# Three dense PSUM banks in a hybrid encoder kernel, with the retention's scores and outputs in one bank

## The chip, the cores and the metric

The kernel runs on one core of a Trainium2 chip. A core has five engines with a queue of instructions each: TensorE (PE in the profile; its weight loads are shown apart, as PEld), VectorE (DVE), ScalarE (ACT), GpSimd (POOL) and SyncE (SP), which issues the DMAs here. Each engine takes its instructions in the order of its queue. An instruction can wait for semaphores that other engines or DMAs raise. TensorE writes its products into PSUM, a memory of eight banks; a bank holds 512 columns of 32-bit floats on each of 128 partitions. VectorE and ScalarE read the products there.

The metric is the device time of one execution in microseconds (us): the median over the runs.

## The reference, cut to what matters

Two layers are computed over 2048 tokens of width 1024. Each normalizes its input, projects it to eight parts of 512 columns, runs two kinds of heads, and adds the projected result to the input.

```python
def hybrid_layer(x, norm_gain, w_in, w_out, rel_bias, cos, sin):
    hn = rms_norm(x, norm_gain)
    proj = hn @ w_in
    aq, ak, av, ag, rq, rk, rv, rg = jnp.split(proj, cuts, axis=-1)
    ya = chunked_rel_attention(aq, ak, av, rel_bias)      # 8 heads x 64, softmax over 9 chunks of 64
    yr = chunkwise_retention(rq, rk, rv, cos, sin)        # 4 heads x 128
    y = concatenate([ya * silu(ag), yr * silu(rg)])
    return x + y @ w_out

def chunkwise_retention(q, k, v, cos, sin):               # q, k turned by rotary phases
    att = einsum("bnihd,bnjhd->bnhij", qc, kc) * intra_decay     # scores, masked with decays
    o_intra = einsum("bnhij,bnjhe->bnihe", att, vc)
    kv = einsum("bnjhd,hj,bnjhe->bnhde", kc, k_decay, vc)
    state = state * chunk_decay + kv                             # carried from chunk to chunk
    o_inter = einsum("bnihd,hi,bnhde->bnihe", qc, q_decay, states)
    return rms_norm(o_intra + o_inter)
```

## The kernel before, in words

**Precision.** Every large operand is held as two 16-bit floats, an upper part and a remainder (`h` and `l`). A product of two such operands takes three TensorE instructions: upper by upper, upper by remainder, remainder by upper.

**Tiles and stages.** A layer is worked through in four groups `s` (one retention head and two attention heads each), and a group in four stages `n` of 512 tokens. A stage has two dense parts. `dense_T` makes four sections `j` of 128 transposed columns (attention's q and k, retention's q and k): 24 products of 128x512 each, into one PSUM tile per section. `dense_V` makes the untransposed columns (v, gates, retention's v) for four blocks `a` of 128 tokens: 24 products of 128x512 each. After the four groups `wout` does the output projection with the same shape of product (line 1105) into the same pool of banks.

**Steps.** All these are Python generators that yield after eight wide products. `run` goes around them. At each step it lets the dense generator issue its products, then calls `tick`, which issues what an earlier step had put off with `later(k, ...)` until k steps on, then lets `attention` issue its part, then pulls work from a list of background generators (the preparation of the next group's weights, the first layer's norms). The order on the four compute engines' queues is the order in which the Python code issues. Attention of stage n runs beside the dense parts of stage n+1, in eight units (four blocks `a`, two heads `hx`) of three steps.

**The retention in these steps.** Unit (a, 1) issues the attention scores S (lines 800, 801) at its first step. At its second step `decayed` issues three products of 128x128 (line 860): the retention's scores of block a+1, or of the next stage's block 0. At its third step `retention` issues the outputs of block a: six products into columns 0 to 127 and three, the addition to the state, into columns 128 to 255. With `tick`, VectorE multiplies the scores by the decay mask one step after they were issued (line 880), ScalarE makes the upper half of the masked scores two steps after (line 864), VectorE the remainder three steps after (line 868). After the outputs, VectorE adds to the state one step on (line 908), ScalarE squares the outputs for the norm two steps on (line 929, into columns 256 to 383 of the same tile), VectorE and GpSimd make the root three steps on, and VectorE the normalized, gated result four steps on (line 925).

**PSUM.** Eight banks: pool `psD` has two for the dense sections, `psS` one tile of two banks for attention's scores, `psR` four for everything small: attention's outputs `o` (line 817), the retention's scores `r1` (line 873), its outputs `r2` (line 891), the sums over columns that the weight preparation takes (`allsum`, line 322) and the start's transposes. A pool hands out its banks in turn; the first write to a tile waits until the last reader of the tile that had the bank before is done. So a section of `dense_T` or `dense_V` waits for the reading of the section two before it; the last reader of a `dense_V` section is VectorE's gate (line 770).

**The first group's tokens.** In the first layer's first group the transposed tokens of stage n+1 are made while stage n runs: for each of four blocks of 128 tokens a norm, a split into upper half and remainder, and two transposing DMAs (lines 236 and 237), by the generator `norms_from_input` and, for the second stage, a list written out by hand. A wide product of `dense_T` reads all four blocks. Stage (0, 0, 0) alone has its first two sections in column parts (line 712): products of 128 columns, one block of tokens at a time.

Of the kernel before, what the change touches and what calls it, by code (L numbers as in the profile page):

```python
# [10 lines left out]
F32 = mybir.dt.float32  # L11
I32 = mybir.dt.int32
AF = mybir.ActivationFunctionType
ALU = mybir.AluOpType
AX = mybir.AxisListType
PSUM = bass.MemoryType.PSUM
DRAM = bass.MemoryType.DRAM

P = 128
# [8 lines left out]
def hybrid_trunk(ctx: ExitStack, tc: tile.TileContext, x, pos, gain, gcol, w_in, w_out, rel, fgain,  # L28
# [4 lines left out]
    KT = D // P  # L33
# [3 lines left out]
    act, dve, pool, pe, sp = nc.scalar, nc.vector, nc.gpsimd, nc.tensor, nc.sync  # L37
# [8 lines left out]
    w4 = ctx.enter_context(tc.tile_pool(name="w4", bufs=3))  # L46
    gp = ctx.enter_context(tc.tile_pool(name="gp", bufs=5))
    dp = ctx.enter_context(tc.tile_pool(name="dp", bufs=1, space=DRAM))
    psD = ctx.enter_context(tc.tile_pool(name="psD", bufs=2, space=PSUM))
    psS = ctx.enter_context(tc.tile_pool(name="psS", bufs=1, space=PSUM))  # L50
    psR = ctx.enter_context(tc.tile_pool(name="psR", bufs=4, space=PSUM))


    warm = cp.tile([P, 1], F32, tag="warm", name="warm")
# [146 lines left out]
    ring = {}  # L201
# [393 lines left out]
    def later(k, fn):  # L595
        deferred.append([k, fn])
# [11 lines left out]
    def dense_T(l, s, n, g, st):  # L608
        hh, hl = hT[l, n]
        nm = f"{l}_{s}_{n}"  # L610
        st.tabc = b1.tile([P, 512], F32, tag="tabc", name=f"tabc{nm}")
        st.tabs = b1.tile([P, 512], F32, tag="tabs", name=f"tabs{nm}")
        def tab_load():
            while n not in tab_done:
                pull(1)
            sp.dma_start(st.tabc, tab_d[n][0])
            sp.dma_start(st.tabs, tab_d[n][1])

        first = (l, s, n) == (0, 0, 0)
# [85 lines left out]
        if first:  # L705
            ps = [psD.tile([P, 512], F32, tag="dense", name=f"dT{nm}_{j}") for j in range(2)]
            for (j, a) in ((0, 0), (0, 1), (0, 2), (1, 0), (1, 1), (1, 2), (0, 3), (1, 3)):
                cs = slice(a * P, (a + 1) * P)
                m = 0
# [5 lines left out]
            for j in range(2):  # L715
                evacuate(j, ps[j])
                yield
        for j in range(2 if first else 0, 4):
            if j == 2 and not first:
                tab_load()  # L720
            if first:
                ps = psR.tile([P, 512], F32, tag="small", name=f"dT{nm}_{j}")
            else:
                ps = psD.tile([P, 512], F32, tag="dense", name=f"dT{nm}_{j}")
            while g.tdone <= j:
                pull(1)
            m = 0
            terms = ((g.h, hh), (g.l, hh), (g.h, hl))
            order = [(kt, w) for w in terms for kt in range(KT)] if j == 0 else [(kt, w) for kt in range(KT) for w in terms]
            for kt, (w_, h_) in order:  # L730
                pe.matmul(ps, w_[:, j, kt, :], h_[:, kt, :], start=(m == 0), stop=(m == 23))  # L731
                m += 1
                if m in (8, 16) or (m == 24 and first):
                    yield
            evacuate(j, ps)
            yield
# [41 lines left out]
    def attention(l, s, n, g, st, prev, nxt):  # L778
# [61 lines left out]
        for i, (a, hx) in enumerate(units):  # L840
            flow(1)
            u = qk(a, hx)
            yield
            if hx == 1:
                if a < 3:
                    decayed(l, s, n, g, st, a + 1)
                elif nxt is not None:
                    decayed(*nxt, 0)
            yield
            if hx == 1:  # L850
                next(ret, None)
            elif a == 0 and (l, s, n) == (0, 0, 0):
                decayed(l, s, n, g, st, 0)
            pipe.append(lambda u=u: pv(u))
            yield


    def products(out_, pairs):
        for i, (w_, m_) in enumerate(pairs):
            pe.matmul(out_, w_, m_, start=(i == 0), stop=(i + 1 == len(pairs)))  # L860

    def upper_of(dst, src):

        act.activation(dst[:, 0], src, AF.Copy, scale=2.0 ** -11)

    def rest_of(dst, src):

        dve.scalar_tensor_tensor(out=dst[:, 1], in0=dst[:, 0], scalar=-2.0 ** 11, in1=src, op0=ALU.mult, op1=ALU.add)

    def decayed(l, s, n, g, st, a):  # L870
        nm = f"{l}_{s}_{4 * n + a}"
        cs = slice(a * P, (a + 1) * P)
        r1 = psR.tile([P, 512], F32, tag="small", name=f"r1{nm}")
        products(r1[:, 0:P], [(st.rk[:, i, cs], st.rq[:, j, cs]) for i, j in ((0, 0), (0, 1), (1, 0))])

        def upper():
            st.dT = b1.tile([P, 2, P], F16, tag="dT", name=f"dT{nm}")
            upper_of(st.dT, r1[:, P:2 * P])

        later(1, lambda: dve.tensor_tensor(r1[:, P:2 * P], r1[:, 0:P], g.msk, op=ALU.mult))  # L880
        later(2, upper)
        later(3, lambda: rest_of(st.dT, r1[:, P:2 * P]))

    def retention(l, s, n, g, st):
        for a in range(4):
            t = 4 * n + a
            nm = f"{l}_{s}_{t}"
            cs = slice(a * P, (a + 1) * P)
            last = t == NT - 1
            dT = st.dT  # L890
            r2 = psR.tile([P, 512], F32, tag="small", name=f"r2{nm}")
            rv = st.rv[a]
            terms = [(dT[:, 0], rv[:, 0]), (dT[:, 0], rv[:, 1])]
            if t > 0:
                sh = ring["halves"]
                terms += [(st.rq[:, 0, cs], sh[:, 0]), (st.rq[:, 1, cs], sh[:, 0]), (st.rq[:, 2, cs], sh[:, 1])]
            products(r2[:, 0:P], terms + [(dT[:, 1], rv[:, 2])])
            if not last:
                kh, kl = st.kt[:, a, :], st.kt[:, 4 + a, :]
                products(r2[:, P:2 * P], [(kh, rv[:, 0]), (kh, rv[:, 1]), (kl, rv[:, 0])])  # L900
                if t == 0:
                    ring["state"] = b1.tile([P, P], F32, tag="state", name=f"state{nm}")
                ns = ring["state"]
                sh = ring["halves"] = b1.tile([P, 2, P], F16, tag="sh", name=f"sh{nm}")

                def add(r2=r2, ns=ns, t=t):
                    if t > 0:
                        dve.scalar_tensor_tensor(out=ns, in0=r2[:, P:2 * P], scalar=2.0 ** (-7 - s), in1=ns,
                                                 op0=ALU.mult, op1=ALU.add)
                    else:  # L910
                        dve.tensor_scalar(ns, r2[:, P:2 * P], 2.0 ** (-7 - s), None, op0=ALU.mult)

                later(1, add)
                later(2, lambda sh=sh, ns=ns: upper_of(sh, ns))
                later(3, lambda sh=sh, ns=ns: rest_of(sh, ns))
                later(5, lambda ns=ns: act.activation(ns, ns, AF.Copy, scale=(1.0 - 2.0 ** (-5 - s)) ** P))
            ss = b2.tile([P, 1], F32, tag="rss", name=f"rss{nm}")

            def root(ss=ss):
                dve.tensor_scalar(ss, ss, g.ra[:, 0:1], g.re[:, 0:1], op0=ALU.mult, op1=ALU.add)  # L920
                pool.tensor_tensor(ss, ss, mhalf, op=ALU.pow)

            def fin(t=t, a=a, r2=r2, ss=ss, nm=nm):
                y = b1.tile([P, P], F32, tag="yr", name=f"yr{nm}")
                dve.scalar_tensor_tensor(out=y, in0=r2[:, 0:P], scalar=ss[:, 0:1], in1=st.g[a][:, P:256],
                                         op0=ALU.mult, op1=ALU.mult)
                sp.dma_start(y_d[t][:, 512 + s * P:512 + (s + 1) * P], y)

            later(2, lambda r2=r2, ss=ss: act.activation(r2[:, 2 * P:3 * P], r2[:, 0:P], AF.Square,
                                                         accum_out=ss))  # L930
            later(3, root)
            later(4, fin)
            yield
# [197 lines left out]
    def pull(k):  # L1131
        for _ in range(k):
            while bg:
                try:
                    next(bg[0][0])
                    bg[0][1] -= 1
                    break
                except StopIteration:
                    bg.pop(0)
# [7 lines left out]
    def grp(l, s):  # L1147
        if (l, s) not in groups:
            groups[l, s] = Grp()
        return groups[l, s]  # L1150
# [146 lines left out]
    spare = [h_.rearrange("p k c -> p (k c)")[:, i * 2 * D:(i + 1) * 2 * D] for h_ in far[1] for i in range(2)]  # L1297
    xk = [Tok(t, xs0[t], None) if t < 4 else Tok(t, late[t - 4], spare[t - 4]) for t in range(8)]
    d0 = dense_T(0, 0, 0, g00, st0)
    g00.vh = b3.tile([P, KT, 512], F16, tag="wh", name="whV0_0")  # L1300
    g00.vl = b3.tile([P, KT, 512], F16, tag="wl", name="wlV0_0")
# [69 lines left out]
    for l in range(DEPTH):  # L1371
        gO = [Grp(), Grp()]
        go = Grp()
        for s in range(NSW):
            g = grp(l, s)
            for n in range(NS):
                first = (l, s, n) == (0, 0, 0)
                if not first:
                    st = states.setdefault((l, s, n), St())
                    dT = dense_T(l, s, n, g, st)  # L1380
                else:
                    st = st0
# [42 lines left out]
                m = n + 1 if n + 1 < NS else 0  # L1425
# [90 lines left out]
```

## Time and profile before

| | us |
|---|---|
| median of 3 runs (lowest, highest) | 2094.98 (2092.48, 2095.95) |
| the profiled execution | 2094.75 |
| its span, from the first to the last instruction | 2092.8 |
| TensorE busy | 2004.4 (96%) |
| VectorE busy | 1343.8 (64%) |
| ScalarE busy | 1141.3 (55%) |
| GpSimd busy | 432.9 (21%) |
| DMA queue q1, share of 16 engines | 66.4% |
| mean granted TensorE clock | 0.991 |

The profile names a group of instructions by line, engine, operation and tiles written and read (out<-in). The name `r` stands for both tiles of the retention, `r1` and `r2`, since numbers are left out; products that read `rot` only are scores, those that begin with `rv,dT` are outputs. In a group's row stand the count, the busy time in us, the mean duration of one in ns, and the idle time of the engine just before these instructions with what ended most of it. In the order of time a row begins with the start and the duration in us; in square brackets stands the idle time before it and what released it.

### The profile page before, as it was taken

The numbers are of one execution on the slowest core, as the hardware profiler recorded it, in microseconds if no ns is written. First come the engines' busy times: TensorE is split into PE (matmuls) and PEld (weight loads), VectorE is DVE, ScalarE is ACT, GpSimd is POOL, SyncE is SP. The second block draws the span as 40 slices with busy tenths as digits, with TensorE's granted clock in tenths as the row PEclk, the third lists the DMA queues.
The fourth block names the chain that finished last, engine by engine and source line by source line (L and its number), as shares of the span: only waits on it lengthen the run. The fifth ranks groups of instructions, "written<-read, shape, count | busy, mean of one in ns | idle before, by whom it ended". The sixth has DMA issues, their size and how long they took to land.

```text
span 2092.8 us, 39599 instructions
## 1 busy us (share of the span) xinstructions
PE 2004.4 (96%) x14014; PEld 1049.4 (50%) x14014; DVE 1343.8 (64%) x4031; ACT 1141.3 (55%) x2522; POOL 432.9 (21%) x509
## 2 busy tenths in 40 slices
PE   6888999999999999998999999999999999998998
PEld 4344455555555555444444555555555555554443
DVE  7676666666656666576654666666666667656643
ACT  7455665556565654455444546554655565455432
POOL 1022222222122212121000222222222222222100
PEclk9999999999999999999999999999999999999999
DMA  8767674557476764599965556655655776558874
GB/s 247 171 127 162 136 166 114 115 112 159 110 169 133 161 166 99 113 211 260 219 185 113 120 102 142 130 121 106 155 123 118 178 156 162 117 100 183 212 199 123
DMA packets 645702, 313.65 MB, mean 150 GB/s; under 512 B 459232, under 2 KB 602080, under 8 KB 645504
## 3 DMA queue, kind: packets, MB, share of 16 engines
q1 hardware_dynamic: 645504, 311.12, 66.4%
q8 instruction: 110, 1.80, 0.4%
q14 instruction: 88, 0.72, 0.1%
HBM read 123.26 MB, written 41.98 MB: 79 GB/s over the span
## 4 chain that ended last, share of the span: by engine, by line
PE 55%; DMA 7%; DVE 5%; ACT 3%; issue 1%; SPq 1%; POOL 0%; POOLq 0%; DVEq 0%; ACTq 0%
PE dT L731 18%; PE dV L752 15%; PE dO L1105 12%; DMA pT<-pq 2%; PE r L860 2%; PE S L801 2%; PE S L800 2%; PE o L820 1%; PE o L821 1%; PE o L822 1%; DVE sc L804 1%; DMA swp<-rot 1%; DMA yhy<-rhy 1%; ACT sc L807 1%; ACT pq L809 1%
## 5 line engine op out<-in xcount | busy, mean ns | idle before, releaser
L810 POOL TENSOR_TENSOR pq<-sc,pq 128x640 f16<-128x640 f32 (+4 forms) x256 | 323.8, 1265 | 1175.9 <-issue 590.7
L807 ACT ACTIVATE sc<-sc,mq,cT 128x640 f32<-128x640 f32 (+4 forms) x256 | 218.5, 853 | 558.1 <-DVE mq L806 413.7
L752 PE MATMUL dV<-whV,hTh 128*128 128x512 f16 x1024 | 354.5, 382 | 13.0 <-DVE gt L770 12.8
L731 PE MATMUL dT<-hTh,whT 128*128 128x512 f16 x1008 | 349.4, 382 | 14.7 <-DMA hTh<-hTl 9.6
L752 PE MATMUL dV<-wlV,hTh 128*128 128x512 f16 x1024 | 354.1, 381 | 0.0
L752 PE MATMUL dV<-whV,hTl 128*128 128x512 f16 x1024 | 354.0, 381 | 0.0
L731 PE MATMUL dT<-hTl,whT 128*128 128x512 f16 x1008 | 346.6, 379 | 0.0
L731 PE MATMUL dT<-hTh,wlT 128*128 128x512 f16 x1008 | 346.6, 379 | 0.0
L752 PEld LDWEIGHTS <-hTh 128*128 128x128 f16 x2048 | 197.3, 98 | 227.7 <-DVE gt L770 16.4
L731 PEld LDWEIGHTS <-whT 128*128 128x128 f16 x2016 | 192.9, 98 | 221.6 <-issue 24.1
L804 DVE CUSTOM_DVE_ANT_0 sc<-S,bias 128x640 f32<-128x640 f32 (+4 forms) x256 | 188.4, 736 | 78.8 <-PE S L801 61.1
L1105 PE MATMUL dO<-whO,yly 128*128 128x512 f16 x512 | 194.1, 379 | 2.4 <-DMA yly<-rly 2.4
L1105 PE MATMUL dO<-whO,yhy 128*128 128x512 f16 x512 | 194.0, 379 | 1.2 <-DVE gt L770 0.6
L1105 PE MATMUL dO<-wlO,yhy 128*128 128x512 f16 x512 | 194.0, 379 | 0.0
L809 ACT ACTIVATE pq<-sc 128x640 f16<-128x640 f32 (+4 forms) x256 | 171.5, 670 | 10.9 <-DMA pT<-pq 3.0
L1105 PEld LDWEIGHTS <-yhy 128*128 128x128 f16 x1024 | 99.6, 98 | 115.1 <-issue 0.8
L752 PEld LDWEIGHTS <-hTl 128*128 128x128 f16 x1024 | 99.7, 98 | 105.0 <-issue 2.8
L800 PE MATMUL S<-k,q 128*128 128x128 f16 (+3 forms) x592 | 143.1, 268 | 7.9 <-DVE mq L804 7.9
L731 PEld LDWEIGHTS <-wlT 128*128 128x128 f16 x1008 | 97.2, 98 | 101.8 <-issue 1.1
L820 PE MATMUL o<-v,pT 128*128 128x65 f16 x1120 | 129.6, 193 | 10.2 <-DMA pT<-pq 9.7
L801 PE MATMUL S<-k,q 128*128 128x128 f16 (+3 forms) x592 | 130.5, 268 | 0.0
L820 PEld LDWEIGHTS <-pT 128*128 128x128 f16 x1120 | 105.3, 97 | 49.2 <-DMA pT<-pq 21.3
(350 smaller groups left out, 3352.7 us busy)
## 6 DMA issues: line engine op xcount, KB each, us to landing
q<-qq SPq DMA_DIRECT2D x128, 128.0 KB, 2.7
yyy<-y_d SPq DMA_DIRECT2D x32, 512.0 KB, 4.6
stT<-in_w_in_dram SPq DMA_DIRECT2D x27, 512.0 KB, 4.8
stV<-in_w_in_dram SPq DMA_DIRECT2D x26, 512.0 KB, 4.5
k<-kk SPq DMA_DIRECT2D x128, 64.0 KB, 2.0
swp<-rot SPq DMA_DIRECT2D x64, 128.0 KB, 2.5
tabc<-tab SPq DMA_DIRECT2D x32, 256.0 KB, 2.7
tabs<-tab SPq DMA_DIRECT2D x32, 256.0 KB, 2.9
```

Of the source, the lines that this page charges most:

```text
L731: pe.matmul(ps, w_[:, j, kt, :], h_[:, kt, :], start=(m == 0), stop=(m == 23))
L752: pe.matmul(ps, h_[:, kt, a * P:(a + 1) * P], w_[:, kt, :], start=(m == 0), stop=(m == 23))
L800: pe.matmul(o, st.q[:, hx, 0, cs], k_, start=True, stop=False)
L801: pe.matmul(o, st.q[:, hx, 1, cs], k_, start=False, stop=True)
L804: dve.tensor_tensor_reduce(out=v, in0=S[:, 0:w], in1=g.bias[hx][:, 640 - w:640], scale=1.0, scalar=-3.0e38, op0=ALU.add, op1=ALU.max, accu ...
L807: act.activation(v, v, AF.Exp, bias=m[:, 0:1], scale=g.c[:, 0:1])
L809: act.activation(pq[:, 0:w], v, AF.Copy)
L810: pool.tensor_tensor(pq[:, w:2 * w], v, pq[:, 0:w], op=ALU.subtract)
L820: pe.matmul(o[:, 0:65], u.p[:, b, :], v_[:, 0:65], start=(b == 0), stop=False)
L821: pe.matmul(o[:, 0:64], u.p[:, b, :], v_[:, 65:129], start=False, stop=False)
L860: pe.matmul(out_, w_, m_, start=(i == 0), stop=(i + 1 == len(pairs)))
L1105: pe.matmul(ps, h_[:, kt, :], w_[:, kt, :], start=(m == 0), stop=(m == 23))
```

## The change

The pool `psD` gets a third bank and `psR` loses its fourth. The retention's outputs of block a no longer take a bank of their own: they go into the bank that the scores of block a+1 were given one step before, kept in `ring["rr"]`. The scores move to its last 128 columns and are masked in place; the outputs keep columns 0 to 383. Only the very last block's outputs take a new bank.

In the first group of the first layer, the stages n = 1, 2 and 3 compute the first two sections of `dense_T` in column parts: for each of the four token blocks, 24 products of 128x128 for section 0 and then 24 for section 1, into two dense banks that are held side by side. They yield every 32 products, so that the count of steps stays at twelve a stage. Both sections are evacuated after the last block.

```diff
-    psD = ctx.enter_context(tc.tile_pool(name="psD", bufs=2, space=PSUM))
+    psD = ctx.enter_context(tc.tile_pool(name="psD", bufs=3, space=PSUM))
-    psR = ctx.enter_context(tc.tile_pool(name="psR", bufs=4, space=PSUM))
+    psR = ctx.enter_context(tc.tile_pool(name="psR", bufs=3, space=PSUM))
...
+        second = (l, s) == (0, 0) and n > 0
+        if second:
+            ps = [psD.tile([P, 512], F32, tag="dense", name=f"dT{nm}_{j}") for j in range(2)]
+            m = 0
+            for (j, a) in ((j, a) for a in range(4) for j in range(2)):
+                while g.tdone <= j:
+                    pull(1)
+                cs = slice(a * P, (a + 1) * P)
+                for i, (w_, h_) in enumerate((w_, h_) for (w_, h_) in ((g.h, hh), (g.l, hh), (g.h, hl)) for kt in range(KT)):
+                    kt = i % KT
+                    pe.matmul(ps[j][:, cs], w_[:, j, kt, :], h_[:, kt, cs], start=(i == 0), stop=(i == 23))
+                    m += 1
+                    if m % 32 == 0 and m < 192:
+                        yield
+                if a == 3:
+                    evacuate(j, ps[j])
+            yield
-        for j in range(2 if first else 0, 4):
+        for j in range(2 if first or second else 0, 4):
...
     def decayed(l, s, n, g, st, a):
-        r1 = psR.tile([P, 512], F32, tag="small", name=f"r1{nm}")
-        products(r1[:, 0:P], [(st.rk[:, i, cs], st.rq[:, j, cs]) for i, j in ((0, 0), (0, 1), (1, 0))])
+        ring["rr"] = psR.tile([P, 512], F32, tag="small", name=f"r1{nm}")
+        r1 = ring["rr"][:, 3 * P:4 * P]
+        products(r1, [(st.rk[:, i, cs], st.rq[:, j, cs]) for i, j in ((0, 0), (0, 1), (1, 0))])
...
-            upper_of(st.dT, r1[:, P:2 * P])
+            upper_of(st.dT, r1)
-        later(1, lambda: dve.tensor_tensor(r1[:, P:2 * P], r1[:, 0:P], g.msk, op=ALU.mult))
+        later(1, lambda: dve.tensor_tensor(r1, r1, g.msk, op=ALU.mult))
         later(2, upper)
-        later(3, lambda: rest_of(st.dT, r1[:, P:2 * P]))
+        later(3, lambda: rest_of(st.dT, r1))
...
     def retention(l, s, n, g, st):
-            r2 = psR.tile([P, 512], F32, tag="small", name=f"r2{nm}")
+            r2 = ring.pop("rr", None)
+            if r2 is None:
+                r2 = psR.tile([P, 512], F32, tag="small", name=f"r2{nm}")
```

## The prediction

> **What bounds the kernel now.** I read the share of busy time, then TensorE's groups by line (columns: count, busy us and mean ns of one, idle us before and what ended it), then the order of time around the lines that the change touches.
>
> ```profile
> span 2092.8 us, 39599 instructions
> PE 2004.4 (96%) x14014; PEld 1049.4 (50%) x14014; DVE 1343.8 (64%) x4031; ACT 1141.3 (55%) x2522; POOL 432.9 (21%) x509
> L752 PE MATMUL dV<-whV,hTh 128*128 128x512 f16 x1024 | 354.5, 382 | 13.0 <-DVE gt L770 12.8
> L731 PE MATMUL dT<-hTh,whT 128*128 128x512 f16 x1008 | 349.4, 382 | 14.7 <-DMA hTh<-hTl 9.6 <-DMA hTh<-rhn 2.8 <-issue 2.2
> L1105 PE MATMUL dO<-whO,yhy 128*128 128x512 f16 x512 | 194.0, 379 | 1.2 <-DVE gt L770 0.6 <-DMA yyy<-y_d 0.6
> L800 PE MATMUL S<-k,q 128*128 128x128 f16 (+3 forms) x592 | 143.1, 268 | 7.9 <-DVE mq L804 7.9
> ```
>
> TensorE is busy 96% of the span. All that the change can win is idle time of TensorE: 12.8 + 0.6 us waiting for a dense bank whose last reader is VectorE's gate (L770), and 14.7 us waiting for transposed tokens before a T stage. Every wait newly put on TensorE is paid in full, since nothing else stands ready on its queue.
>
> **The change, part by part.** *A third dense bank.* The 13.4 us above go, and a third bank costs nothing on any engine: −13.4.
>
> *One bank for a block's outputs and the next block's scores.* This part decides. `decayed` issues the three score products of block a+1; one step (eight wide products) later `retention` issues the outputs of block a. These had a bank each. Now they have one, and in the built program the first output product waits for VectorE's masking (L880) of the scores written one step before: 126 of 128 outputs carry this wait, which none had. VectorE only has that one step to do it. The trace of before holds both instants, since it issues the same work in the same order:
>
> ```profile
> 91.25 0.29 DVE L880 TENSOR_TENSOR r<-r,msk 128x128 f32<-128x128 f32 x1
> 91.57 0.33 PE L860 MATMUL r<-rv,dT 128*128 128x128 f16 x3
> ...
> 872.04 0.28 PE L860 MATMUL r<-rv,dT 128*128 128x128 f16 x2
> 884.63 0.29 DVE L880 TENSOR_TENSOR r<-r,msk 128x128 f32<-128x128 f32 x1
> ...
> 1249.06 0.35 DVE L925 SCALAR_TENSOR_TENSOR yr<-r,rss,gt 128x128 f32<-128x128 f32 x1 [0.66 <-POOL rss L921]
> 1249.86 0.82 DVE L804 CUSTOM_DVE_ANT_0 sc<-S,bias 128x640 f32<-128x640 f32 x1 [0.45 <-PE S L801]
> 1251.39 0.33 PE L860 MATMUL r<-rot,rot 128*128 128x128 f16 x3
> 1252.89 1.92 DVE L670 TENSOR_TENSOR rot<-rot,tabc 128x512 f32<-128x512 f32 x1 [1.95 <-DMA y_d<-yr]
> 1253.28 0.28 PE L860 MATMUL r<-rv,dT 128*128 128x128 f16 x2
> 1255.91 0.29 DVE L880 TENSOR_TENSOR r<-r,msk 128x128 f32<-128x128 f32 x1
> ...
> 1306.78 0.28 PE L860 MATMUL r<-rv,dT 128*128 128x128 f16 x2
> 1312.60 0.29 DVE L880 TENSOR_TENSOR r<-r,msk 128x128 f32<-128x128 f32 x1
> 1319.83 0.28 PE L860 MATMUL r<-rv,dT 128*128 128x128 f16 x2
> 1323.15 0.29 DVE L880 TENSOR_TENSOR r<-r,msk 128x128 f32<-128x128 f32 x1
> ...
> 1946.33 0.28 PE L860 MATMUL r<-rv,dT 128*128 128x128 f16 x2
> 1949.36 0.29 DVE L880 TENSOR_TENSOR r<-r,msk 128x128 f32<-128x128 f32 x1
> ```
>
> Lag = end of the masking minus start of the output: −0.03 at 91.57 us, 12.88 at 872, 2.92 at 1253, 6.11 at 1306, 3.61 at 1319, 3.32 at the last. Over the 126 pairs (first and last above), 96 have a positive lag, 290 us in sum. That is the upper end: every lag arises anew.
>
> It need not, since a stalled TensorE lets VectorE catch up. So I carried each stall forward as a lead, cut to the least time by which any VectorE instruction before the next masking started after the product it reads: where VectorE itself stands waiting for a later product, the lead is gone.
>
> ```profile
> DVE sc L804 <- PE S L801: 61.1, 85, 2.5
> ```
>
> VectorE waited 85 times for attention scores alone. It did at 1249.86, one block's work behind the last output; the lag of 2.92 at 1253 then came from a tile that arrived late (1252.89), so it comes again whatever was stalled before. Between 1306 and 1319 VectorE never ran dry: the 3.61 is covered by the 6.11 paid before. Block by block this leaves 73 stalls, 206 us, the lower end. As a lead is lost to ScalarE's and DMA's waits too, I take 215.
>
> *The clock after a stall.*
>
> ```profile
> 78.91 3.26 PE L731 MATMUL dT<-hTh,whT 128*128 128x512 f16 x8 [9.64 <-DMA hTh<-hTl]
> 140.13 1.89 PE L731 MATMUL dT<-hTh,whT 128*128 128x512 f16 x8 [2.21 <-issue]
> 204.59:208.01 3.41, 3.11 (x8) 1.20 (x9) 1.08 (x4) 1.68 (x7) 1.40 (x1) 0.50 0.86 174
> sum 34.13, PE 23.39 PEld 9.93 DVE 18.57 ACT 16.33 POOL 6.07; mean PE 3.90 PEld 1.66 DVE 3.09 ACT 2.72 POOL 1.01
> ```
>
> After an idle 9.64 us eight products took 3.26 us, after 2.21 us only 1.89; after 2.8 us (in the T row above) the granted clock was 0.50. The last line sums the six half-clock stretches behind such gaps: TensorE was busy 23.39 us in them, so lost about 11.7, or 1.95 each. Of the 73 stalls 26 exceed 2.81 us, ten of them by under 0.6: I count 21, +41. Lower end: the 16 above 3.4 us at 1.4 (the shortest busy time, 2.81, halved), 22; upper end: all 44 lags above 2.81, 86. [...]
>
> *Cross waits in the shared bank.* VectorE's state update (L908) now waits for ScalarE's copy of the masked scores, and ScalarE's Square (L929) for VectorE's remainder. In the trace 28 updates start before that copy ends (20 us in sum), 13 Squares before that remainder (9 us); the worst update, and its block's Square:
>
> ```profile
> 1269.29 0.28 DVE L908 SCALAR_TENSOR_TENSOR state<-r,state 128x128 f32<-128x128 f32 x1
> 1270.73 0.26 ACT L864 ACTIVATE dT<-r 128x128 f16<-128x128 f32 x1
> 1272.58 0.28 DVE L868 SCALAR_TENSOR_TENSOR dT<-dT,r 128x128 f16<-128x128 f16 x1
> 1272.76 0.26 ACT L929 ACTIVATE r<-r 128x128 f32<-128x128 f32 x1
> ```
>
> The copy ends 1.70 us after the update began, the remainder 0.10 us after the Square did. Queued behind an update are the next scores' maximum (L804) and the next masking; behind a Square, the next exponentials. TensorE pays only what reaches its next wait: 0 to 29, taken 5. [...]
>
> *Three banks instead of four for the small tiles.* Per block two attention outputs and one shared bank are taken: three, as many as there are. A score product comes one full turn after the bank's former use ended with the norm (L925): in the rows above that norm is done at 1249.41, the scores come at 1251.39. Only the column sums of the weight preparation break the turn: ten of them would meet a norm still to come, 8 us in all, here 1.61:
>
> ```profile
> 571.21 0.17 PE L323 MATMUL msT<-mbT,ones 128*128 128x1 bf16 x1
> 572.47 0.35 DVE L925 SCALAR_TENSOR_TENSOR yr<-r,rss,gt 128x128 f32<-128x128 f32 x1
> ```
>
> Bounds 0 and 8, taken 5.
>
> *Column parts.* In three stages 144 wide products become 576 of 128 columns. The first stage has such:
>
> ```profile
> 30.73 0.61 PE L712 MATMUL dT<-hTl,whT 128*128 128x128 f16 x8
> 31.18 0.61 PE L712 MATMUL dT<-hTh,wlT 128*128 128x128 f16 x8
> 86.04 0.23 PE L860 MATMUL r<-rot,rot 128*128 128x128 f16 x1 [0.20 <-DVE rot L676]
> ```
>
> Eight start in 0.45 us, so four take 0.223 us against 0.216 for one wide (1.73 us for eight): +1.1 us. For it the work starts at the first token block instead of the last. But of the 9.6 us little can be had: the first scores come three steps into that stage and need VectorE's rotated keys, ready at 86.0 (last row) after a swap that no product of this stage feeds. TensorE would run half the parts early and stand there instead; I take 1.5 won, near the lower end of 0 to 9.6. The 2.2 and 2.8 us go, behind earlier parts or stalls: −6.5 of 14.7 (0 to 14.7).
>
> *What falls in the shadow.* Of the 7.9 us before S, 6.5 stand some 6 us behind the two largest lags (at 872 and 1885 us), where VectorE will have caught up: −6.5 (0 to −7.9). Most of the old half-clock stretches go with their gaps: −8 of 11.7.
>
> **Sum**, against the profiled execution's own 2094.75 us (span 2092.8 and 1.95 around it; the median is 2094.98, so no correction): 215 + 41 + 5 + 5 + 1.1 − 13.4 − 6.5 − 6.5 − 8 = +232.7, that is 2327. Lower ends together: 206 + 22 + 1.1 − 13.4 − 14.7 − 7.9 − 11.7 = +181, 2276; upper: 290 + 86 + 29 + 8 + 1.1 − 13.4 = +401, 2496.
>
> **Rivals.** *One debt, paid once (faster).* If VectorE is merely behind as a whole, the first large stall gives it a lead that it never loses; TensorE pays the largest lag only, 12.9 us at 872, and wins 13.4 + 14.7 us of idle time: 2080. It decides if VectorE doesn't run dry between outputs. For: lags follow each other (1306, 1319). Against: 85 waits for S. That the shared bank brings no wait at all (the build's waits being met long before) would give about the same; 96 late pairs of 126. Together 0.04.
>
> *A lead that lasts a stage.* If VectorE keeps what it gained through the four blocks of a stage, each stage pays its largest lag: 161 us over 32 stages; with 20 for the clock and the same other terms, 2094.75 + 161 + 20 − 23 = 2253. 0.09.
>
> *The norm becomes a second wait.* The norm (L925) is the shared bank's last reader; its chain runs over ScalarE, VectorE and GpSimd, and now has the Square's wait in it. If it slips beyond the next scores by 1 us in 120 blocks: 2327 + 120 = 2447. Above it has 2.0 us in hand, and a stall moves the output and the next scores alike, so 0.05.
>
> **How the numbers follow.** Forecast 0.82, rivals 0.04, 0.09, 0.05. Time: the likeliest, 2327. The range 2240 to 2440 takes the lasting lead in and most of the way to the upper ends, which won't all meet; it leaves out the fast case and the far tail. A measurement of this kernel tells 0.2% (4 us) from no change. Faster 0.03, same 0.01 (the fast case with a few us more of stalls), slower 0.96.
>
> **What would show it.** Right: a group of output products (line of L860) idle some 200 us, released by the masking; about 70 such waits, 15 to 45 half-clock stretches; no idle time before dV put down to the gate; L731's gaps of 9.6 us moved to the score products. Wrong: fewer than 100 us there; large idle time before score products released by the norm (third rival); or the first 126 waits closing within 20 us in all (first rival).

## The result and the profile after

| | before | after |
|---|---|---|
| median, us (lowest, highest; 4 runs each on the same chip) | 2093.84 (2092.48, 2095.95) | 2304.65 (2300.17, 2310.97) |
| ratio, with its 95% interval | | 1.1008 (1.0979 to 1.1037) |
| the profiled execution, us | 2094.75 | 2303.62 |
| its span, us | 2092.8 | 2301.5 |

The change makes the kernel a tenth slower: 210.8 us between the medians, 208.7 between the spans. Lines of the file have moved: the retention's products stand on L877 (L860 before), the masking on L898 (L880), the wide products on L748 and L769 (L731 and L752).

The head of the page of after and its row of the granted clock (tenths, 40 slices):

```profile
span 2301.5 us, 40327 instructions
...
PE 2064.1 (90%) x14446; PEld 1096.4 (48%) x14446; DVE 1355.7 (59%) x4031; ACT 1145.0 (50%) x2522; POOL 438.2 (19%) x509
...
PEclk9898989999999999989999999999999999998999
```

Two things grew. TensorE was busy for 59.7 us more (2004.4 before) with nearly the same products, and idle for 149.0 us more (span less busy: 88.4 before, 237.4 after). VectorE's own work hardly changed (1343.8, now 1355.7). TensorE's groups by line (busy, mean ns of one, idle before them and its releaser) say where the idle time is:

```profile
L769 PE MATMUL dV<-whV,hTh 128*128 128x512 f16 x1024 | 378.3, 409 | 0.0
L748 PE MATMUL dT<-hTh,whT 128*128 128x512 f16 x960 | 335.3, 383 | 0.0
L817 PE MATMUL S<-k,q 128*128 128x128 f16 (+3 forms) x592 | 143.5, 268 | 0.0
L837 PE MATMUL o<-v,pT 128*128 128x65 f16 x1120 | 132.0, 195 | 0.0
L877 PE MATMUL r<-rv,dT 128*128 128x128 f16 x384 | 66.7, 234 | 200.7 <-DVE r L898 199.3 <-ACT raw L662 0.7
L877 PE MATMUL r<-rot,rot 128*128 128x128 f16 x384 | 42.7, 220 | 5.9 <-ACT rot L673 5.1 <-DVE rot L676 0.8
L728 PE MATMUL dT<-hTh,whT 128*128 128x128 f16 x192 | 15.6, 228 | 0.0
```

The first of the retention's output products stand still for 199.3 us behind the masking. The four largest of the old waits are gone: 13.0 us before the dV products, 14.7 before the T products and 7.9 before S are now 0.0, and so are 10.2 us before the attention outputs. Some 38 us of idle time stand elsewhere, as before (42.6 then), in small pieces; the largest in the rows above are 5.9 us before the scores. The waits by engine (us in total, times, longest) count the new stall:

```profile
ACT sc L824 <- DVE mq L823: 563.5, 199, 6.1
...
DVE sc L821 <- PE S L818: 206.2, 147, 4.5
PE r L877 <- DVE r L898: 199.3, 72, 12.1
```

72 waits. VectorE in its turn now stands 147 times waiting for attention scores, 206.2 us (85 times and 61.1 before): the two wait for each other in turn. The longest stall in the order of time, the counterpart of the pair at 872 us before:

```profile
968.28 0.33 PE L877 MATMUL r<-rot,rot 128*128 128x128 f16 x3
...
969.17 0.35 DVE L945 SCALAR_TENSOR_TENSOR yr<-r,rss,gt 128x128 f32<-128x128 f32 x1
...
974.70 0.82 DVE L821 CUSTOM_DVE_ANT_0 sc<-S,bias 128x640 f32<-128x640 f32 x1 [4.58 <-DMA yhy<-rhy]
...
980.25 1.28 DVE L233 SCALAR_TENSOR_TENSOR rly<-yyy,sy,rhy 128x1024 f16<-128x1024 f32 x1 [2.58 <-DMA yly<-rly]
981.45 0.68 DVE L670 TENSOR_TENSOR raw<-raw,swp 128x512 f32<-128x512 f32 x1
982.05 0.29 DVE L898 TENSOR_TENSOR r<-r,msk 128x128 f32<-128x128 f32 x1
...
982.40 0.37 PE L877 MATMUL r<-rv,dT 128*128 128x128 f16 x2 [12.06 <-DVE r L898]
```

The scores began at 968.28, and the mask, which takes 0.29 us, came 13.8 us later. It isn't the mask that is slow: in VectorE's queue other instructions stand ahead of it. By the profile two of them waited for transposing DMAs (4.58 and 2.58 us); nearly all of the rest is work of their own (VectorE was busy for 6.39 of the 13.77 us). Before, TensorE did not care; now it pays for what stands ahead of the mask.

The extra busy time is the clock. Stretches of the records at half clock in after, the first, one with a long stall and the last with work in it (length, then each engine's busy time, the granted clock, DMA share and GB/s), and the sum of all 37:

```profile
24.29:27.71 3.42, 3.42 (x36) 3.42 (x34) 2.33 (x3) 3.42 (x6) 0.00 (x0) 0.50 1.07 358
...
973.20:986.85 13.65, 4.45 (x20) 2.25 (x20) 7.02 (x20) 5.93 (x11) 1.40 (x1) 0.50 0.63 130
...
2154.21:2157.62 3.41, 3.41 (x15) 1.51 (x13) 1.16 (x2) 0.28 (x1) 0.00 (x0) 0.50 0.93 173
...
sum 195.10, PE 135.32 PEld 74.83 DVE 82.29 ACT 55.66 POOL 12.50; mean PE 3.66 PEld 2.02 DVE 2.22 ACT 1.50 POOL 0.34
```

The last of the 37 lies behind all products. In the other 36 TensorE was busy for 135.3 us at a granted clock of 0.50, so by estimate it lost half of that, 67.7 us, where before lost 11.7: 56.0 of the 59.7.

### The profile page after: what moved, and what is told of

It is laid out like the page before. It is cut to its first block, busy times and chain, and to the rows that moved or that the text cites. A ratio compares the mean times of both kernels' runs of the same rounds, so it can differ in the third digit from the quotient of the medians.

```text
span 2301.5 us, 40327 instructions
## 1 busy us (share of the span) xinstructions
PE 2064.1 (90%) x14446; PEld 1096.4 (48%) x14446; DVE 1355.7 (59%) x4031; ACT 1145.0 (50%) x2522; POOL 438.2 (19%) x509
## 3 DMA queue, kind: packets, MB, share of 16 engines
q1 hardware_dynamic: 645504, 311.12, 59.7%
## 4 chain that ended last, share of the span: by engine, by line
PE 34%; DVE 10%; ACT 6%; issue 3%; DMA 3%; SPq 1%; POOL 1%; DVEq 0%; POOLq 0%; ACTq 0%
PE dO L1125 12%; PE dT L748 9%; PE dV L769 8%; DVE sc L821 2%; PE r L877 2%; ACT sc L824 2%; DMA swp<-rot 1%; ACT pq L826 1%; PE S L818 1%; PE S L817 1%; DVE swp L670 1%; DVE rl L844 1%; DVE raw L670 1%; DVE rot L670 1%; DVE mq L823 1%
## 5 line engine op out<-in xcount | busy, mean ns | idle before, releaser
L769 PE MATMUL dV<-whV,hTh 128*128 128x512 f16 x1024 | 378.3, 409 | 0.0
L769 PE MATMUL dV<-whV,hTl 128*128 128x512 f16 x1024 | 357.0, 384 | 0.0
L769 PE MATMUL dV<-wlV,hTh 128*128 128x512 f16 x1024 | 355.8, 383 | 0.0
L748 PE MATMUL dT<-hTh,whT 128*128 128x512 f16 x960 | 335.3, 383 | 0.0
L748 PE MATMUL dT<-hTh,wlT 128*128 128x512 f16 x960 | 334.0, 381 | 0.0
L748 PE MATMUL dT<-hTl,whT 128*128 128x512 f16 x960 | 333.3, 381 | 0.0
L821 DVE CUSTOM_DVE_ANT_0 sc<-S,bias 128x640 f32<-128x640 f32 (+4 forms) x256 | 188.7, 737 | 243.1 <-PE S L818 206.2
L769 PEld LDWEIGHTS <-hTh 128*128 128x128 f16 x2048 | 204.2, 102 | 227.1 <-issue 34.4
L748 PEld LDWEIGHTS <-whT 128*128 128x128 f16 x1920 | 184.0, 98 | 194.4 <-issue 6.7
L877 PE MATMUL r<-rv,dT 128*128 128x128 f16 x384 | 66.7, 234 | 200.7 <-DVE r L898 199.3
L1125 PEld LDWEIGHTS <-yhy 128*128 128x128 f16 x1024 | 100.9, 99 | 115.8 <-issue 4.0
L877 PEld LDWEIGHTS <-dT 128*128 128x128 f16 x384 | 38.6, 101 | 242.7 <-issue 222.4
L769 PEld LDWEIGHTS <-hTl 128*128 128x128 f16 x1024 | 100.5, 99 | 106.6 <-issue 4.6
L817 PE MATMUL S<-k,q 128*128 128x128 f16 (+3 forms) x592 | 143.5, 268 | 0.0
L748 PEld LDWEIGHTS <-wlT 128*128 128x128 f16 x960 | 93.0, 98 | 98.3 <-issue 2.8
```

The source lines that it names most:

```text
L769: pe.matmul(ps, h_[:, kt, a * P:(a + 1) * P], w_[:, kt, :], start=(m == 0), stop=(m == 23))
L817: pe.matmul(o, st.q[:, hx, 0, cs], k_, start=True, stop=False)
L821: dve.tensor_tensor_reduce(out=v, in0=S[:, 0:w], in1=g.bias[hx][:, 640 - w:640], scale=1.0, scalar=-3.0e38, op0=ALU.add, op1=ALU.max, accu ...
L1125: pe.matmul(ps, h_[:, kt, :], w_[:, kt, :], start=(m == 0), stop=(m == 23))
```

## The experiments

The theory under test: the masking in the shared bank is the whole cost, anew in each block, with the half clock that its stalls bring. The medians of the kernel before, taken beside the versions, lie between 2093.84 and 2099.78 us, so each version is given with its ratio to the one taken beside it.

**Sharing alone.** Two dense and four small banks, no column parts; only the bank is shared.

```diff
-    psD = ctx.enter_context(tc.tile_pool(name="psD", bufs=3, space=PSUM))
+    psD = ctx.enter_context(tc.tile_pool(name="psD", bufs=2, space=PSUM))
-    psR = ctx.enter_context(tc.tile_pool(name="psR", bufs=3, space=PSUM))
+    psR = ctx.enter_context(tc.tile_pool(name="psR", bufs=4, space=PSUM))
-        second = (l, s) == (0, 0) and n > 0
+        second = False
```

> The shared bank alone: two dense banks and four small ones as before, no column parts. Theory M (the outputs wait on VectorE's masking of the next block's scores): some 2310 us (2295 to 2330), again about 70 waits of the output products for the masking, 190 to 210 us in sum, and a half clock behind the longer ones; that the dense banks are two again adds little, since VectorE catches up in the stalls. Rival R (three small banks in place of four are too few): within 5 us of before, since there are four.

Measured: 2316.23 us, ratio 1.1043 (1.1025 to 1.1062). Its groups by line:

```profile
L769 PE MATMUL dV<-whV,hTh 128*128 128x512 f16 x1024 | 382.2, 413 | 0.0
L748 PE MATMUL dT<-hTh,whT 128*128 128x512 f16 x1008 | 352.2, 385 | 11.3 <-DMA hTh<-hTl 9.4 <-DMA hTh<-rhn 1.9
...
L877 PE MATMUL r<-rv,dT 128*128 128x128 f16 x384 | 66.0, 232 | 208.3 <-DVE r L898 197.9 <-ACT whT L330 9.6
```

The sharing alone costs as much as the whole change, with four small banks: rival R is out. And look at the first row: with only two dense banks no dV product waits for the gate any more. This fits stalls on the masking that give VectorE the time that it lacked there.

**Third bank and sharing, no column parts.** After with `second = False` alone.

> The changed kernel without column parts: third dense bank and shared bank stay. Theory (stalls on the masking set nearly all of the time, the third dense bank is worth the 13.4 us that TensorE waited for the gate, the column parts next to nothing): 2298 to 2312 us, masking waits 190 to 205 us. Rival 1 (the column parts cost as they do alone, 5 to 10 us): 2290 to 2298 us. Rival 2 (the stalls already cover the gate's wait, so that the third bank brings nothing): within 4 us of the version with sharing alone, about 2312 to 2322 us.

Measured: 2318.88 us, ratio 1.1035 (1.1006 to 1.1063), 207.5 us of idle time put to the masking (73 waits). The last rival is right: beside the sharing, the third bank brings nothing that can be told (1.1043 without it, 1.1035 with it). After stands 0.3% lower than this version, 1.1008, but the intervals overlap; whether the column parts win those 6 us beside the sharing stays open.

**Masking at once.** The masking is issued right behind its scores instead of a step later; nothing else of after changes.

```diff
-        later(1, lambda: dve.tensor_tensor(r1, r1, g.msk, op=ALU.mult))
+        dve.tensor_tensor(r1, r1, g.msk, op=ALU.mult)
```

> The changed kernel with the mask issued at once behind the scores instead of a step later, so that background work and the attention output's scaling come behind it on VectorE's queue. By the trace of before the lags sum to 224 us in place of 290. Theory M: the waits of the outputs shrink in that proportion, from 199 to 140 to 170 us, and the time to 2235 to 2275 us. A theory in which the wait is not set by what stands ahead of the mask on VectorE: 2300 us, unchanged.

Measured: 2238.54 us, ratio 1.0681 (1.0661 to 1.0702). The wait and the group:

```profile
PE r L877 <- DVE r L898: 127.1, 43, 7.7
```

```profile
L877 PE MATMUL r<-rv,dT 128*128 128x128 f16 x384 | 65.3, 230 | 145.1 <-DVE r L898 127.1 <-DVE omaxO L506 10.3 <-DVE m2T L325 5.1
```

A place one step earlier in VectorE's queue takes 72 us off the wait and a third of the loss with it. The time came as expected; the wait fell further than the 140 to 170 us, and 18 us of idle time stand before the same products for other reasons (1.4 in after). The dose moves the answer: it is the mask's place in the queue that sets the price.

**Scores and outputs in one step.** `decayed` moves one step later, to directly before `retention`, so that scores and outputs follow each other on TensorE and the mask comes behind both. Three versions: with the rest of the change (`together`), without column parts, and with two dense and four small banks and no column parts.

```diff
             yield
+            yield
             if hx == 1:
...
                     decayed(*nxt, 0)
-            yield
-            if hx == 1:
                 next(ret, None)
```

> The changed kernel, but with the next block's scores and this block's outputs issued in one step, so that no VectorE instruction on the bank stands between them on TensorE's queue; three dense banks, column parts, the shared bank and three small banks stay. Theory M: the outputs wait for nothing, and with the dense banks' idle time (13 us) and most of that before the T stages gone the time is 2070 to 2090 us, under both kernels. Rival R (three small banks): 2290 us or more. Rival C (in a shared bank ScalarE and VectorE wait for each other, and that sets the time): 2250 us or more, since the sharing stays.

> As the one-step kernel, without the column parts. Theory M: 2075 to 2095 us, the column parts being worth 2 to 10 us once nothing else stalls. Rivals R and C: 2250 us or more.

> As the one-step kernel, with two dense banks and four small ones and without column parts: the sharing is all that is left. Theory M: within 6 us of before (2088 to 2100 us), the idle time before dV back at 10 to 13 us. Rival C: 2250 us or more. Rival R says the same as M.

Measured: 2123.30 (1.0127, 1.0113 to 1.0141), 2120.46 (1.0115, 1.0100 to 1.0129), 2126.94 (1.0149, 1.0132 to 1.0166). The wait on the masking is gone, and with it 189 of the 219 us by which sharing alone was slower on this chip (the third version against the first experiment). Rivals R and C, which asked for 2250 us or more, are out. But all three stayed above what I had expected, by more than 20 us, and above the kernel before. Groups and waits of the first version:

```profile
L817 PE MATMUL S<-k,q 128*128 128x128 f16 (+3 forms) x592 | 142.6, 267 | 18.6 <-DVE mq L821 18.6
L837 PE MATMUL o<-v,pT 128*128 128x65 f16 x1120 | 130.0, 194 | 24.3 <-DMA pT<-pq 23.2 <-DVE yr L944 1.0
```

```profile
ACT sc L824 <- DVE rl L843: 275.3, 89, 5.6
DVE dT L884 <- ACT r L948: 78.2, 51, 2.1
```

Attention now waits for its transposed probabilities and for the maximum of its scores (23.2 and 18.6 us; 9.7 and 7.9 before). ScalarE's exponentials stand 275.3 us behind VectorE's reading of the attention outputs (100.9 before, 41 times), and VectorE's remainder 78.2 us behind ScalarE's Square, which it meets in the shared bank. The next version tells how much of this is the sharing.

**The new order alone.** The version with two dense banks, but scores and outputs in a bank of their own again:

```diff
-        ring["rr"] = psR.tile([P, 512], F32, tag="small", name=f"r1{nm}")
-        r1 = ring["rr"][:, 3 * P:4 * P]
+        r1 = psR.tile([P, 512], F32, tag="small", name=f"r1{nm}")[:, 3 * P:4 * P]
...
-            r2 = ring.pop("rr", None)
-            if r2 is None:
-                r2 = psR.tile([P, 512], F32, tag="small", name=f"r2{nm}")
+            r2 = psR.tile([P, 512], F32, tag="small", name=f"r2{nm}")
```

> The one-step order of scores and outputs, each with a bank of its own, two dense and four small banks, no column parts: against together_two only the sharing is taken out. What is open is why the one-step kernels still take some 25 us more than before. Theory C (the cross waits in the shared bank: VectorE's remainder behind ScalarE's Square, VectorE's mask behind the outputs, make the softmax and its transposes late): 2090 to 2102 us, waits of ScalarE for VectorE's reciprocal back near 100 us from 275. Rival O (the order itself: the scores come a step later and crowd VectorE): 2118 us or more.

Measured: 2112.26 us, ratio 1.0081 (1.0065 to 1.0096), between the two forecasts: neither was met. The wait that I expected back at 100 us is not:

```profile
ACT sc L824 <- DVE rl L843: 267.3, 89, 4.3
DVE dT L884 <- ACT dT L880: 55.5, 52, 1.6
```

So the loss of 1.5% with two dense banks splits in halves: 0.8%, some 17 us, comes with the later place of the scores, with no bank shared; the other 0.7%, some 14 us, with the sharing. So nearly all of the exponentials' wait comes with the order, not with the sharing. What the sharing adds in waits: VectorE's remainder stands 77.9 us behind the Square with the shared bank (third version), against 55.5 behind ScalarE's copy here, and TensorE is idle 14.5 us longer in all, 8.0 of it before attention outputs whose transposed probabilities come late. That the meetings of ScalarE and VectorE cause all of this is argued from these waits, not shown by a run. Why the later scores hold up the exponentials so much was not taken further.

**Column parts alone.** The kernel before with column parts; the scores also stand in the last columns of their bank and are masked in place, as in after (no run has that alone):

> Before with the column parts alone: two dense, four small banks, scores and outputs in banks of their own. If they win what the idle time before the T stages promised, 2080 to 2085 us; if the first scores' wait for the rotated keys takes its place, as the prediction has it, 2088 to 2096 us, with 5 us of idle time before the first scores.

Measured: 2102.88 us, ratio 1.0036 (1.0022 to 1.0051), a miss. Its groups:

```profile
L748 PE MATMUL dT<-hTh,whT 128*128 128x512 f16 x960 | 331.8, 379 | 2.2 <-DVE qq L634 2.2
L728 PE MATMUL dT<-hTh,whT 128*128 128x128 f16 x192 | 16.1, 232 | 15.4 <-DVE gt L787 15.4
```

The wait for transposed tokens is gone (14.7 us before, now 2.2 for something else), but 15.4 us stand in its place: the two sections take both dense banks at once, and the second bank is free only when the gate of the stage before has read it. With two dense banks the parts don't pay. The other forecast of 5 us before the first scores did not come either: 1.8 us stand before all scores together.

**Scores in the attention output's bank.** Scores are issued right behind the attention outputs of the same step and go into that tile's last 128 columns, so that the Square, the state update and the norm are not met there. The outputs of the retention have a bank of their own, and the weight sums go to the dense banks, of which there are three. Copy and remainder stay where they were in time.

```diff
-            o = psR.tile([P, 512], F32, tag="small", name=f"o{u.nm}")
+            o = ring["o"] = psR.tile([P, 512], F32, tag="small", name=f"o{u.nm}")
...
-        ring["rr"] = psR.tile([P, 512], F32, tag="small", name=f"r1{nm}")
-        r1 = ring["rr"][:, 3 * P:4 * P]
+        r1 = ring.get("o")
+        if r1 is None:
+            r1 = psR.tile([P, 512], F32, tag="small", name=f"r1{nm}")
+        r1 = r1[:, 3 * P:4 * P]
...
-        later(2, upper)
-        later(3, lambda: rest_of(st.dT, r1))
+        later(2 + d, upper)
+        later(3 + d, lambda: rest_of(st.dT, r1))
```

> A way to free the eighth bank without the wait: the next block's scores ride in the bank of the attention output that is issued just before them (same step, and only VectorE's reads follow before ScalarE's copy, which waits for the mask anyway); the retention's outputs keep a bank of their own, the weight sums take dense banks. Three dense and three small banks, column parts. Theory M and C: no output waits for a mask and no new wait between ScalarE and VectorE; of the waits that three small banks bring, the trace of before puts 16 attention outputs behind a remainder by 24 us in sum at most: 2075 to 2100 us. Rival (any sharing of a bank costs some 25 us or more): 2110 us or more.

> The version whose scores ride in the attention output's bank, without column parts. Theory (its remaining cost is the attention output that waits for the remainder of the scores, about 30 us, and the columns are worth 0 to 3 us): 2109 to 2117 us, 25 to 35 us idle before the attention outputs (L837's counterpart) released by the remainder. Rival (the columns cost 5 to 10 us here as they do alone): 2102 to 2108 us.

Measured: 2113.32 us, ratio 1.0086 (1.0069 to 1.0102), with column parts; 2110.80, ratio 1.0053 (1.0037 to 1.0070), without. The second one's group before which TensorE stands longest:

```profile
L837 PE MATMUL o<-v,pT 128*128 128x65 f16 x1120 | 129.9, 193 | 46.0 <-DVE dT L887 28.4 <-DVE rl L843 8.1 <-DMA pT<-pq 6.7
```

The wait has moved once more. The bank is now read last by the remainder of the scores, some four steps after it was filled, and the attention outputs that take it next wait 28.4 us for that. The first of the two missed what I had expected of it: the rival's 2110 us or more was right as a number, though the loss, 17 us, is less than the 25 that it gave as the reason. The second came as expected. In this pair, too, the column parts won nothing.

**Third dense bank without sharing.** Scores, outputs and both attention outputs use the three small banks, each with a tile of its own; the weight sums go to the dense banks; no column parts.

> Third dense bank, no sharing, no column parts: the retention's scores and outputs and both attention outputs take turns in the three small banks, each with a bank of its own; the weight preparation's column sums take dense banks. Theory (a wait that comes anew in each block is paid anew: the attention outputs fall due before the readers two to three uses back are done, 63 us of lateness behind the gated attention output, 24 behind the remainder, 16 behind the norm by the order of the kernel before): 100 to 140 us over the kernel before, 2195 to 2235 us, half-clock stretches 10 to 30. Rival (a debt paid once a stage, or VectorE catching up): 20 to 60 us over, 2115 to 2155 us. If it is below both kernels, the sharing wasn't needed for the third bank.

Measured: 2130.15 us, ratio 1.0148 (1.0131 to 1.0164). The rival is right, not the theory (11 stretches at half clock, with work in them, were within the theory's 10 to 30).

```profile
L769 PE MATMUL dV<-whV,hTh 128*128 128x512 f16 x1024 | 353.4, 381 | 0.6 <-DVE m2T L325 0.6
...
L837 PE MATMUL o<-v,pT 128*128 128x65 f16 x1120 | 130.3, 194 | 67.6 <-DVE ya L849 39.0 <-DVE dT L885 12.6 <-DMA pT<-pq 9.7
...
L877 PE MATMUL r<-rv,dT 128*128 128x128 f16 x384 | 61.9, 219 | 2.8 <-DVE yr L942 2.8
```

The order of time of before has these three readers late by 63, 24 and 16 us; 39.0, 12.6 and 2.8 us were paid. So about half of the lateness was paid; that the rest was covered by stalls paid earlier is the likely reading. The third dense bank does take its 12.8 us away (first row), and its price is 57 us more before the attention outputs; over all, with other waits gone, TensorE is idle 26 us longer than before (114.6 against 88.4). Also: the sharing wasn't needed for it, and three small banks without sharing cost a seventh of what the shared bank does.

None of these versions is faster than the kernel before.

## Why the prediction came out as it did

The forecast, 2327 us, stands 23 above the profiled execution, and its mechanism is the one that the runs show. Term by term:

- *Waits on the masking.* Taken 215 us in 73 stalls, measured 199.3 in 72; the largest lag, 12.88 us, came as a stall of 12.06. The lower end, 206, would have been the better value: the 9 us that I added for leads lost to ScalarE's and DMA's waits didn't come.
- *Half clock: the size was off.* Taken +41 less 8, that is +33; measured +56.0. The price of one stretch was right (1.95; 67.7 in 36 stretches is 1.88). The count failed, 21 against 36. One of the 36 lies in the start, one behind the 5.1 us before the first scores, and 34 behind stalls on the masking; 11 of these 34 follow stalls of only 2.00 to 2.56 us. I had read a least gap of 2.8 us from the trace of before; the runs don't show one, since in after a stall of 2.00 us was followed by half clock and one of 2.87 was not (last section). Nor does a run show the 3.4 us by which the lower end counts: 16 of the 34 follow stalls of 2.00 to 3.13 us.
- *What falls in the shadow: the size was off.* Taken −13.4 − 6.5 − 6.5 = −26.4; the four old waits named with the groups above, 45.8 us, are all gone. The 9.7 us before the attention outputs that waited for transposed probabilities I hadn't counted at all.
- *Third dense bank.* −13.4 was put down to the wrong cause. The wait for the gate did go, but sharing alone takes it away with two banks. With the bank for itself the kernel wins those 12.8 us, and loses more elsewhere.
- *Column parts.* Of the 9.6 us I let 1.5 be won; in after 5.9 us stand before the first scores, which wait for the rotated keys, as the prediction said they would, so 3.7 were won. That the parts need two dense banks at once, the prediction did not see: alone they cost 0.4%.
- *Cross waits in the shared bank, and the norm.* Taken 5 each. The cross waits came: VectorE's update waits for ScalarE's copy 47 times, 37.1 us in sum (28 times and 20 us by the old order), and the Square 6 times, 8.2 us, for the remainder. What of this TensorE pays can't be told beside the stalls; in the one-step order the sharing costs some 14 us, inside the 0 to 29 given. No idle time of TensorE in after is put to the norm, but the reason given was wrong. The text ahead of the prediction has the small banks handed out in turn, and the prediction has the scores come a full turn after the norm, 2.0 us in hand in the one row shown. In the trace of before 56 norms of two blocks earlier end only after the scores began, by 80 us in sum; in strict turn that would have been the term, not 8. The banks aren't handed out so: in the rows above the scores began at 968.28, and the norm of two blocks earlier, at 969.17, was still to come; 19 scores of after are like this, and none waits for it.

In sum: idle time was to grow by 198.6 us (215 + 5 + 5 − 26.4) and grew by 149.0; busy time was to grow by 34.1 (33 and 1.1 for the parts) and grew by 59.7. Two errors of opposite sign, 50 and 26 us, leave the 24; that the forecast came within about 1% is in part luck.

Of the rivals, the debt paid once is refuted by 72 stalls, among them one of 11.94 us as late as 2092 us; the lead that lasts a stage foresaw 161 us of waits and falls short; the norm as a second wait did not appear.

## What to carry to other kernels

As this program is built, a product that goes into a bank waits for the readers of all that the bank held, whatever columns they read (here outputs in columns 0 to 255 for the masking of columns 384 to 511: 199.3 us in 72 waits). So two tiles in one bank tie together the readers of both, and on engines that take their work in order the tie reaches to everything queued ahead of those readers (a mask of 0.29 us came 13.8 us after its scores): the price can be read beforehand from the old order of time, as end of the reader minus start of the next writer, block by block, with a lead carried only as far as the reader's engine doesn't run dry (206 us read so, 199.3 measured). A long new stall hides the short old ones (45.8 us of them in after), so what a change wins by removing an old wait must not be counted again if it also adds a stall ahead of it. When scores, outputs and their readers were moved here, the wait moved to another reader or another engine (28.4 us behind the remainder with the scores in the attention output's bank, 39.0 behind the gated attention output with three small banks and no sharing); list who frees each bank last before choosing which to merge, and take the banks from the built program, not from the order in which they are asked for.

## What the runs showed of the hardware

I had not expected that the length of a single gap does not tell whether half clock follows it. In the trace of after the 37 stretches at half clock are 3.41 us long, or two or four times that (the last, which ends behind all work, aside), and their starts lie whole multiples of 3.41 us apart. Four stretches of that length in step with them, two pairs of neighbours (length, TensorE's busy time first, the granted clock behind the engines):

```profile
433.89:437.31 3.42, 1.29 (x13) 0.89 (x13) 2.91 (x6) 0.52 (x2) 1.00 (x2) 1.00 0.22 50
437.31:440.72 3.41, 3.41 (x25) 1.99 (x23) 0.01 (x1) 0.00 (x0) 0.00 (x0) 0.50 0.71 142
1416.93:1420.34 3.41, 1.43 (x14) 0.95 (x14) 2.23 (x8) 1.40 (x5) 0.93 (x1) 1.00 1.13 271
1420.34:1423.76 3.42, 3.42 (x35) 1.99 (x34) 1.31 (x6) 0.00 (x0) 0.00 (x0) 1.00 0.87 195
```

With 1.29 us of work in the stretch at 433.89, the next ran at half clock, though TensorE was busy all through it; with 1.43 us in the one at 1416.93, the next ran at full. Single gaps before the output products went both ways: one of 2.00 us that ended at 771 us and one of 2.81 at 955 were followed by half clock, one of 2.81 at 2067 and one of 2.87 at 247 were not. The latter two lie across one of these steps, with 1.57 and 2.00 us in the longer part; the former two lie within one, but for 0.07 us. So the likely reading of this trace is that it matters how much idle time falls into one step. Of the gaps of 3.13 us and more, from 77 us on, each was followed by half clock.
